# The last products of a matrix multiplication: a new order, C21's last part in two column halves, stores by halves on two queues

**The chip, the cores and the metric.** One core of one Trainium2 chip. The metric is device microseconds of one execution, as the median of several runs. The profile of one execution adds the span, from the first to the last instruction, which is about 1.8 us shorter than the time. TensorE is called PE in profile lines, VectorE DVE, ScalarE ACT, GpSimd POOL and SyncE SP; a q behind a name (SPq) is the sequencer of that engine, which waits, branches and issues DMAs.

## The reference

```python
"x": np.random.randn(8, 2048, 2048).astype(np.float32)
"w": np.random.randn(2048, 2048).astype(np.float32)

cs = np.cumsum(x, axis=1)
diff = cs - np.concatenate([zeros, cs[:, :-1, :]], axis=1)   # zeros: one row
return np.matmul(diff, w).astype(np.float32)
```

The difference of the cumulative sum is x again up to rounding, so the kernel computes x @ w.

## The kernel before

The product is done by a Strassen-like scheme with seven products in place of eight, twice nested: blocks A11 … S4 of x against B11 … T4 of w, and inside the last outer product a second level with products `a11 t11` … `s3 Q3`. A product of the inner level is four matmuls of 512 columns into one PSUM bank. ScalarE moves a first result to the output tile with a scale (`keep`), VectorE adds the further ones (`add`).

```python
    def product_in(ps, a, b, first):
        for k in range(4):
            nc.tensor.matmul(
                ps, a[k], b[k], start=(first and k == 0), stop=(k == 3), skip_group_check=True
            )
    ...
    def keep(dst, ps, scale):     # ScalarE: dst = ps * scale
    def add(dst, ps, scale):      # VectorE: dst = ps * scale + dst
    ... (bodies cut)

        def four_last():
            a11, a12, a22, s1, s2, s3, s4 = A4
            Q1, Q2, Q4, t11, Q3, t21, t22 = in4
            C21g, C21h = new_c(b), new_c(c)
            product_in(q, a11, t11, True)
            keep(C21g[:, :NB], q, vg)
            product_in(X[0], a12, t21, False)
            add(C21g[:, :NB], X[0], vg)
            product_in(X[1], s4, t22, False)
            keep(C21g[:, NB:], X[1], vg)
            product_in(e, s1, Q1, True)
            add(C21g[:, NB:], e, vg)
            keep(C21h[:, NB:], Y[1], vh)
            add(C21h[:, NB:], e, vh)
            product_in(q, s2, Q2, False)
            add(C21g[:, NB:], q, vg)
            put(C21g, g + 1, 0)
            product_in(Y[0], a22, Q4, False)
            keep(C21h[:, :NB], Y[0], vh)
            product_in(q, s3, Q3, False)
            for n in range(2):
                at = ds(n * NB, NB)
                add(C21h[:, at], q, vh)
                nc.scalar.dma_start(out2[ds((h + 1) * P, P), at], C21h[:, at])
```

`four_last` is the last function to run. q, e, X[0], X[1], Y[0] and Y[1] are PSUM banks; X and Y already hold partial sums. NB is 512, P is 128. Two early places matter later: seven output stores of 256 KB are issued on GpSimd's queue, at 59 to 64 us, and nine on SyncE's, at 74 to 80 us (the recorded expectations say "about 100 us"):

```python
        with tc.issue_after(whole_max.ins):
            for c, rows, columns in done:
                put(c, rows, columns)                                  # GpSimd's queue
        ...
        for c, rows, columns in done:
            after("sp", lambda: put(c, rows, columns, nc.sync))        # SyncE's queue
```

## Time and profile before

| | kernel before |
|---|---|
| time, median of 3 (lowest to highest) | 1509.28 us (1508.52 to 1510.85) |
| span of the profiled execution | 1507.3 us, granted clock 1.0 (the share of TensorE's full speed that it was given) |
| TensorE, VectorE, ScalarE busy | 99%, 73%, 57% |
| start of the first product of `four_last`, a11 t11 | 1495.56 us |

I measure the end of the kernel from the start of a11 t11, since everything ahead of it is the same in both kernels. This row of TensorE's timeline (start, length, operation, count) sets that zero; it holds a11 t11 and the next product:

```profile
1495.56 1.89 PE L479 MATMUL b<-W,xT 128*128 128x512 f16 x8
```

From there to the end of the span it is 11.8 us, called the *tail* below, 0.8% of the span. The part of it after the last store has landed I call the *closing*.

### The profile page before, as it was taken

The numbers are of one execution on the slowest core, as the hardware profiler recorded it, in microseconds if no ns is written. First come the engines' busy times: TensorE is split into PE (matmuls) and PEld (weight loads), VectorE is DVE, ScalarE is ACT, GpSimd is POOL, SyncE is SP. The second block draws the span as 40 slices with busy tenths as digits, with TensorE's granted clock in tenths as the row PEclk, the third lists the DMA queues.
The fourth block names the chain that finished last, engine by engine and source line by source line (L and its number), as shares of the span: only waits on it lengthen the run. The fifth ranks groups of instructions, "written<-read, shape, count | busy, mean of one in ns | idle before, by whom it ended". The sixth has DMA issues, their size and how long they took to land.

```text
span 1507.3 us, 19123 instructions
## 1 busy us (share of the span) xinstructions
PE 1490.6 (99%) x6911; PEld 673.8 (45%) x6911; DVE 1104.4 (73%) x2053; ACT 864.5 (57%) x1107; POOL 5.2 (0%) x12
## 2 busy tenths in 40 slices
PE   8999999999999999999999999999999999999998
PEld 3444444444444444444444444444444444444443
DVE  7997777776677676777676776766776767776767
ACT  5875655565655566555656555655555565556551
POOL 0100000000000000000000000000000000000000
PEclk9999999999999999999999999999999999999999
DMA  9988878878978987888789788878788888887772
GB/s 362 351 250 233 236 224 246 234 213 227 235 225 244 224 224 236 215 246 236 210 229 232 230 241 217 235 222 248 216 244 207 236 221 250 232 236 216 223 208 112
DMA packets 322479, 351.50 MB, mean 233 GB/s; under 512 B 266896, under 2 KB 266896, under 8 KB 306512
## 3 DMA queue, kind: packets, MB, share of 16 engines
q1 hardware_dynamic: 321536, 347.92, 81.1%
q0 software_dynamic: 560, 1.84, 0.3%
q8 instruction: 54, 0.88, 0.2%
q10 hardware_dynamic: 288, 0.52, 0.1%
q14 instruction: 41, 0.34, 0.1%
HBM read 150.99 MB, written 134.22 MB: 189 GB/s over the span
## 4 chain that ended last, share of the span: by engine, by line
PE 88%; DVE 1%; DMA 1%; issue 0%; ACT 0%; DVEq 0%; ACTq 0%; SPq 0%
PE b L468 52%; PE b L479 36%; DVE c L502 1%; DMA fin<-in_x_dram 0%; DMA xT<-fin 0%; DVE W L511 0%; ACT b L553 0%; DVE W L515 0%; ACT c L497 0%; DVEq L937 0%; DVE xT L511 0%; DVE s L112 0%; DVE m L111 0%; DVE u L586 0%; DVE m L561 0%
## 5 line engine op out<-in xcount | busy, mean ns | idle before, releaser
L502 DVE SCALAR_TENSOR_TENSOR c<-b,u,c 128x512 f32<-128x512 f32 (+1 forms) x883 | 675.0, 799 | 234.8 <-ACT c L497 112.8
L497 ACT ACTIVATE c<-b,u 128x512 f32<-128x512 f32 x496 | 314.5, 680 | 265.4 <-PE b L468 170.5
L468 PE MATMUL b<-W,xT 128*128 128x512 f16 x2048 | 462.1, 379 | 0.8 <-ACT c L497 0.8
L468 PE MATMUL b<-W,W 128*128 128x512 f16 x1764 | 411.7, 379 | 1.8 <-ACT c L497 1.5
L105 ACT ACTIVATE c<-fin 128x2048 f16<-128x2048 f32 x92 | 175.7, 1910 | 242.4 <-DMA out_dram<-c 220.5
L468 PEld LDWEIGHTS <-xT 128*128 128x128 f16 x2048 | 200.4, 98 | 242.6 <-issue 1.1
L468 PEld LDWEIGHTS <-W 128*128 128x128 f16 x2016 | 197.2, 98 | 240.2 <-issue 2.1
L116 ACT ACTIVATE fin<-fin,s 128x2048 f16<-128x2048 f32 x123 | 246.3, 2002 | 93.8 <-issue 50.8
L479 PEld LDWEIGHTS <-W 128*128 128x128 f16 x1560 | 152.1, 98 | 187.5 <-issue 2.5
L479 PE MATMUL b<-W,W 128*128 128x512 f16 x810 | 220.0, 379 | 1.0 <-DVE c L502 1.0
L479 PE MATMUL b<-W,xT 128*128 128x512 f16 x720 | 180.0, 379 | 0.0
L479 PE MATMUL b<-inner,W 128*128 128x512 f16 x660 | 176.2, 379 | 0.0
L479 PEld LDWEIGHTS <-xT 128*128 128x128 f16 x960 | 93.9, 98 | 113.3
L561 DVE TENSOR_REDUCE m<-m 128x1 f32<-128x4 f32 x29 | 4.6, 157 | 106.7 <-ACT b L553 106.7
L553 ACT ACTIVATE b<-fin 128x512 f32<-128x512 f32 x116 | 67.8, 585 | 14.5 <-DMA fin<-in_x_dram 14.5
L468 PE MATMUL b<-W 128*128 128x512 f16 x252 | 75.0, 379 | 0.0
L511 DVE TENSOR_TENSOR W<-W,xT 128x1024 f16<-128x1024 f16 x122 | 68.2, 559 | 3.2
L511 DVE TENSOR_TENSOR W<-xT,W 128x1024 f16<-128x1024 f16 x122 | 67.5, 553 | 0.0
L479 PE MATMUL b<-inner,xT 128*128 128x512 f16 x240 | 61.6, 379 | 0.0
L233 PE MATMUL b<-wb,xP 128*128 128x512 bf16 x240 | 55.4, 383 | 5.9 <-ACT wb L216 4.8
L511 DVE TENSOR_TENSOR W<-xT,xT 128x1024 f16<-128x1024 f16 (+1 forms) x92 | 54.8, 596 | 0.0
L111 DVE TENSOR_SCALAR m<-m 128x1 f32<-128x1 f32 x124 | 18.5, 149 | 34.6 <-ACT c L105 33.5
(54 smaller groups left out, 457.9 us busy)
## 6 DMA issues: line engine op xcount, KB each, us to landing
out_dram<-c SPq DMA_DIRECT2D x247, 512.0 KB, 3.1
fin<-in_x_dram SPq DMA_DIRECT2D x123, 1024.0 KB, 5.5
W<-in_w_dram SPq DMA_DIRECT2D x32, 512.0 KB, 9.6
W<-in_x_dram SPq DMA_DIRECT2D x16, 256.0 KB, 7.4
xT<-fin SPq DMA_TRANSPOSE x184, 5.2
out_dram<-o POOLq DMA_DIRECT2D x7, 256.0 KB, 3.9
out_dram<-o SPq DMA_DIRECT2D x7, 256.0 KB, 4.1
xP<-in_x_dram SPq DMA_DIRECT2D x1, 1024.0 KB, 5.1
```

The source lines that it names most:

```text
L105: return m, nc.scalar.activation(waste.bitcast(f16), xf, ABS, scale=1.0 / ROW, accum_out=m)
L111: nc.vector.tensor_scalar(m, m, TINY, None, MAX)
L116: return xh, nc.scalar.activation(xh, xf, COPY, scale=s)
L233: lambda: nc.tensor.matmul(ps[r][n], xP[:, r, ko, :], wb[h, ko][:, ds(n * NB, NB)], start=(ko == 0), stop=(ko == KO - 1),),
L468: nc.tensor.matmul(ps[n], a[k], b[k][:, n, :], start=(first and k == 0), stop=(k == KH - 1), skip_group_check=True,)
L479: nc.tensor.matmul(ps, a[k], b[k], start=(first and k == 0), stop=(k == 3), skip_group_check=True)
L497: after("act", lambda: nc.scalar.activation(c, p, COPY, scale=scale))
L502: "dve", lambda: nc.vector.scalar_tensor_tensor(c, p, scale, c, MUL, ADD)
L511: after("dve", lambda: nc.vector.tensor_tensor(dst.all, p.all, q.all, op))
L553: lambda: nc.scalar.activation(ps[i % 2], xf[:, at], ABS, scale=1.0 / ROW, accum_out=m4[:, i : i + 1],),
L561: after("dve", lambda: nc.vector.tensor_reduce(m, m4, AX.X, ADD))
```

## The change

Its intent: when the last product is done, little should be left to add and to store. Q4 comes last, cut into two column halves in two banks, so that the last add and store are of 256 columns. The banks are reused later than before, so TensorE need not wait for them. C21g is stored by halves, and the last stores go through two queues.

```diff
             product_in(X[0], a12, t21, False)
             add(C21g[:, :NB], X[0], vg)
-            product_in(X[1], s4, t22, False)
-            keep(C21g[:, NB:], X[1], vg)
+            out_of(C21g, g + 1, ds(0, NB), nc.sync)
+            product_in(q, s2, Q2, False)
+            keep(C21g[:, NB:], q, vg)
             product_in(e, s1, Q1, True)
+            one, two = (ds(n * NB // 2, NB // 2) for n in range(2))
+            keep(C21h[:, two], Y[0][:, two], vh)
+            keep(C21h[:, NB:], Y[1], vh)
+            product_in(X[1], s4, t22, False)
             add(C21g[:, NB:], e, vg)
-            keep(C21h[:, NB:], Y[1], vh)
             add(C21h[:, NB:], e, vh)
-            product_in(q, s2, Q2, False)
-            add(C21g[:, NB:], q, vg)
-            put(C21g, g + 1, 0)
-            product_in(Y[0], a22, Q4, False)
-            keep(C21h[:, :NB], Y[0], vh)
+            add(C21g[:, NB:], X[1], vg)
+            out_of(C21g, g + 1, ds(NB, NB), nc.sync)
             product_in(q, s3, Q3, False)
-            for n in range(2): ...           # two adds of q, two stores of 256 KB on ScalarE's queue
+            keep(C21h[:, one], q[:, one], vh)
+            add(C21h[:, NB:], q, vh)
+            add(C21h[:, two], q[:, two], vh)
+            out_of(C21h, h + 1, ds(NB, NB), nc.scalar)
+            for at, ps, queue in (one, Y[0], nc.sync), (two, X[0], nc.scalar):
+                product_in(ps[:, at], a22, [b[:, at] for b in Q4], ps is X[0])
+                add(C21h[:, at], ps[:, at], vh)
+                out_of(C21h, h + 1, at, queue)
```

(The bodies of the old loop and of `out_of`, which is one `dma_start`, are cut.)

More of the change, by code (lines that the diff above doesn't have):

```diff
@@ L875, in four_last, with out_of @@
             C21g, C21h = new_c(b), new_c(c)
+            def out_of(c, t, at, queue):
+                queue.dma_start(out2[ds(t * P, P), at], c[:, at])
             product_in(q, a11, t11, True)
@@ L879, in four_last @@
             add(C21g[:, :NB], X[0], vg)
+            out_of(C21g, g + 1, ds(0, NB), nc.sync)
+            product_in(q, s2, Q2, False)
+            keep(C21g[:, NB:], q, vg)
+            product_in(e, s1, Q1, True)
+            one, two = (ds(n * NB // 2, NB // 2) for n in range(2))
+            keep(C21h[:, two], Y[0][:, two], vh)
+            keep(C21h[:, NB:], Y[1], vh)
             product_in(X[1], s4, t22, False)
-            keep(C21g[:, NB:], X[1], vg)
-            product_in(e, s1, Q1, True)
             add(C21g[:, NB:], e, vg)
-            keep(C21h[:, NB:], Y[1], vh)
             add(C21h[:, NB:], e, vh)
-            product_in(q, s2, Q2, False)
-            add(C21g[:, NB:], q, vg)
-            put(C21g, g + 1, 0)
-            product_in(Y[0], a22, Q4, False)
-            keep(C21h[:, :NB], Y[0], vh)
-            product_in(q, s3, Q3, False)
-            for n in range(2):
-                at = ds(n * NB, NB)
-                add(C21h[:, at], q, vh)
-                nc.scalar.dma_start(out2[ds((h + 1) * P, P), at], C21h[:, at])
+            add(C21g[:, NB:], X[1], vg)
+            out_of(C21g, g + 1, ds(NB, NB), nc.sync)
+            product_in(q, s3, Q3, False)
+            keep(C21h[:, one], q[:, one], vh)
[6 more added lines that the diff above has]
+                out_of(C21h, h + 1, at, queue)
         inner_product(A3, in3, banks, C12g, C12h, *u, between_3)
```

## The prediction

> **What bounds the kernel now.** I read the page first, to see which engine sets the span, and then only the end, because the change touches nothing but the last function that runs.
>
> The page's busy shares and its chain of waits:
>
> ```profile
> PE 1490.6 (99%) x6911; PEld 673.8 (45%) x6911; DVE 1104.4 (73%) x2053; ACT 864.5 (57%) x1107; POOL 5.2 (0%) x12
> ...
> PE 88%; DVE 1%; DMA 1%; issue 0%; ACT 0%; DVEq 0%; ACTq 0%; SPq 0%
> ```
>
> TensorE (PE) is busy in 99% of 1507.3 us and carries 88% of the chain. The change neither adds nor removes matmul columns (below), so the first 1495 us stay as they are, and what can be won lies after TensorE's stream thins out. The chain from 1495 us on shows where that is (start, length, what):
>
> ```profile
> 1495.72 3.47 PE b L479 x16
> ...
> 1499.28 0.06 DVE c L502
> 1499.34 0.61 issue
> 1499.95 0.14 DVE c L502
> 1500.09 0.51 issue
> 1500.61 0.75 DVE c L502
> 1501.36 0.04 issue
> 1501.40 1.04 PE b L479 x4
> ...
> 1502.53 0.75 DVE c L502
> ```
>
> At 1499.28 the chain leaves TensorE for VectorE (DVE): three adds start 0.66 to 0.67 us apart, and the third must finish reading bank q before the last product, s3 Q3, may accumulate into the same bank. Then come four matmuls, and the final adds. The timelines of TensorE, VectorE and ScalarE (ACT) over the same stretch give starts and lengths:
>
> ```profile
> 1497.29 1.03 PE L479 MATMUL b<-W,W 128*128 128x512 f16 x4
> 1498.15 1.89 PE L479 MATMUL b<-inner,W 128*128 128x512 f16 x8
> 1499.88 1.03 PE L479 MATMUL b<-inner,xT 128*128 128x512 f16 x4
> 1501.40 0.38 PE L479 MATMUL b<-W,W 128*128 128x512 f16 x1 [0.50 <-DVE c L502]
> ...
> 1499.28 2.07 DVE L502 SCALAR_TENSOR_TENSOR c<-b,u,c 128x512 f32<-128x512 f32 x3 [0.81 <-PE b L479]
> 1502.53 1.41 DVE L502 SCALAR_TENSOR_TENSOR c<-b,u,c 128x512 f32<-128x512 f32 x2 [1.18 <-PE b L479]
> ...
> 1496.62 0.69 ACT L497 ACTIVATE c<-b,u 128x512 f32<-128x512 f32 x1 [9.33 <-PE b L479]
> 1498.35 1.26 ACT L497 ACTIVATE c<-b,u 128x512 f32<-128x512 f32 x2 [1.04 <-PE b L479]
> 1500.94 0.69 ACT L497 ACTIVATE c<-b,u 128x512 f32<-128x512 f32 x1 [1.32 <-PE b L479]
> 1503.32 1.00 ACTq L895 DMA_DIRECT2D out_dram<-c  x2
> ```
>
> The bracket of 0.50 us is TensorE waiting for bank q, 1.18 us is VectorE waiting for the last product. VectorE ends at 1502.53 + 1.41 = 1503.94; the second store of 256 KB is issued at 1504.0 (1503.98 from the row of 1.00 us less the 0.34 of one issue). The stores' own view says how long a store takes to land, and the table of stretches when bytes move:
>
> ```profile
> DMA to landing us min/median/max: 2.4/2.4/2.5
> ...
> 1504.00:1506.00 2.00, 0.00 (x0) 0.00 (x0) 0.00 (x0) 0.00 (x0) 0.00 (x0) 1.00 0.68 262
> 1506.00:1507.30 1.30, 0.00 (x0) 0.00 (x0) 0.00 (x0) 0.00 (x0) 0.00 (x0) 0.76 0.00 0
> ```
>
> From 1504.0 no engine works: 3.3 us, 0.22% of the span, is the last store's flight and the program's end. The last one lands at 1503.98 + 2.4 = 1506.4, so some 0.9 us are the closing of the program after it. A finer cut of that view shows the two last stores' bytes moving from about 1504.2 to 1505.6 at some 390 GB/s: 0.67 us for each 256 KB, one after the other.
>
> **What the Trainium skill says.** (1) "PSUM — Partial Sum Buffer", The four PSUM rules: a first matmul clears the written marks of its whole 2 KiB bank, not only of the columns it writes. So the second column half needs a bank of its own when it starts afresh; the change takes X[0], already read. Same page, PSUM bank collisions raise a hardware error: two engines must not be in one bank at once, reads against reads included. The build agrees: the add of q into C21h's right half waits for ScalarE too, though its other operand was settled an add earlier. No run yet shows what that wait costs. (2) "TensorE: Matmul & The Clock Gate", Back-to-back issue gap: N/2.4 + 2.5 ns warm, so 216 ns at 512 columns and 109 ns at 256. The trace agrees at 512: 16 matmuls in 3.62 us, less 0.38 for the last, is 216 ns each. Eight 128-column transposes, each with its own weight load, take 0.61 us, 56 ns apart, so weight loads won't hold 256-column matmuls to more than that. (3) "VectorE: DVE Perf Modes", Why PSUM operands drop a tier: fp32 from PSUM runs at one element a cycle. The trace agrees: adds of 1024 columns take 1272 ns, of 512 take 746, so 1.03 ns a column and 220 ns fixed; a 256-column add is then 0.48 us. (4) "DMA: Bandwidth & Descriptors", Anatomy of one DMA: about 2 us of a DMA are fixed, mostly the write receipt. Landing in 2.4 us with 0.67 us of bytes leaves 1.7 fixed here, for this path.
>
> **The change part by part.** Times are on the old kernel's clock. Columns of matmul: four of 512 in Q4 become eight of 256, the same sum; there are four more weight loads, overlapped. TensorE work saved: none.
>
> a) *Order.* s2 Q2 moves from fifth product to third, so it follows a keep of q by ScalarE, not an add by VectorE. That keep ends at 1496.62 + 0.69 = 1497.31; the matmuls would start at 1497.29, and the old trace shows a release 0.04 us after the reader's end (1501.36 to 1501.40). So they start at 1497.35: +0.06 us. Product e ends as fourth in both orders; its first add moves from 1499.28 to 1499.34.
>
> b) *The wait of TensorE goes.* Starts at four matmuls of 0.216 each: s2 1497.35, e 1498.21, s4 1499.08, s3 1499.94, the two halves of Q4 (four of 0.109) 1500.81 and 1501.24. Before s3, q must have been read: ScalarE keeps s2 from 1498.41 to 1499.10, so no wait. All results are there at 1501.56 + 0.27 = 1501.83 (the tail of a 256-column matmul is my estimate, 0.38 less 0.11), against 1502.05 + 0.38 = 1502.43 in the old kernel. TensorE gains 0.6 us.
>
> c) *ScalarE.* Five keeps in place of four: 512, 512, 256, 512, 256 columns. Starts 0.58 us apart for 512 (1.26 for two). A half is about 0.47 long, 0.37 apart, from 0.83 ns a column (1059 ns for 1024 columns, 1910 for 2048). They end at 1497.31, 1499.10, 1499.5 and 1500.05; the last, of q's left quarter, needs s3, whose last matmul ends at 1500.97, so 1501.02 to 1501.50.
>
> d) *VectorE.* Five last adds (e, e, q, q, q, of 512) become seven: four of 512 and three of 256. After e at 1499.34: the second e waits for the keep of Y[1] (1500.05) and starts at 1500.13; X[1] at 1500.79; q into the right half could start at 1501.46 but waits for ScalarE to leave the bank (1501.50), so 1501.56; then three halves, started 1502.22, 1502.62 and 1503.02 (0.66 after a full one, 0.40 after a half: 0.48 less the same 0.08 overlap). The last ends at 1503.50. Against 1503.94 that is −0.44 us. VectorE has taken TensorE's place: from 1500.8 it runs without a gap while the last product has been ready since 1501.83. That is why the gain is below TensorE's 0.6 plus the shorter last add.
>
> e) *Stores.* The last one has 128 KB, not 256: 0.33 us less of bytes at 390 GB/s. C21g's second half is issued at 1501.5 and C21h's right half at 1502.3, so their bytes are gone by 1503.8; the left quarters follow at 1503.1 on one queue and at 1503.54 on the other. Rows become 1 KB, for which this trace has no record; I put 0.05 us on them. Landing 2.4 − 0.33 + 0.05 = 2.1 us, so 1505.65, plus the 0.9 us of closing: span 1506.55.
>
> Sum: −0.44 (end of VectorE) − 0.28 (shorter last store) = −0.7 to −0.8 us. The predicted time is 1509.28 − 0.8 = **1508.5 us**.
>
> **Rivals.** *VectorE isn't the bound, and the end follows TensorE:* the last half would be added at 1501.93 and finished at 1502.4, a gain of 1.5 at the adds and 0.3 at the store, so 1507.5. Against it: adds of 3 × 0.66 + 3 × 0.40 must still pass after the add of X[1] and cannot start before s4 is done at 1500.1. *The store is hidden anyway:* the end may hang on the closing of the program, or the receipt may not shrink with size; then only the 0.44 remains: 1508.8. For it: 1.7 of the 2.4 us are fixed. *Two queues and small rows cost:* an extra 256-column store, interleaved with the other one in the same DMA engines, could take what it saves; with the 0.44 used up too, 1509.3. *The new waits on ScalarE are longer than worked out,* because five keeps lie on the path of two engines: a keep late by 0.3 us moves VectorE by 0.3, so 1508.8; a whole gain lost gives 1509.3. I see nothing that adds more than 1 us, since every wait of the new order is one keep or one add long.
>
> **Range and chances.** The mechanism is worth 0 to 1.8 us over the rivals, with 0.8 in the middle. The three old runs lie 2.33 us apart (1508.52 to 1510.85), more than the whole effect, and a median of few runs carries perhaps half of that. So the range is **1507.2 to 1509.7**. Two per cent is 30 us, nine times all the time between the last add and the end; no rival comes near: faster 0.005, same 0.99, slower 0.005.
>
> **What would show it.** In the new trace: TensorE's bracket of 0.50 us for VectorE gone, at most 0.1 us for ScalarE before s2; VectorE's last seven adds nearly gapless from 1500.1, the last ending at about 1503.5; 256-column adds of 0.48 us; the add of q released by ScalarE, not TensorE; the last store landing in 2.1 us; the last landing to the span's end 0.9 us. I'm wrong if VectorE has gaps behind TensorE at the end, if the small store lands no sooner than 2.4 us, or if the span falls by more than 1.8 us or not at all. A change before 1495 us would be scatter, not the change.

## The result, and the profile after

The changed kernel took 1509.33 us (median of 3, 1508.78 to 1510.5) against 1509.28. The ratio is 1.000, with a 95% interval of 0.9977 to 1.0023. By the clock on the wall nothing happened. The trace shows that something did.

The timelines of the changed kernel, first TensorE, then VectorE, then ScalarE with its stores:

```profile
1495.68 1.89 PE L479 MATMUL b<-W,xT 128*128 128x512 f16 x8
1497.49 1.89 PE L479 MATMUL b<-inner,W 128*128 128x512 f16 x8
1499.21 1.24 PE L479 MATMUL b<-W,W 128*128 128x512 f16 x5
...
1500.94 1.04 PE L479 MATMUL b<-inner,xT 128*128 128x256 f16 x8
...
1499.48 4.09 DVE L502 SCALAR_TENSOR_TENSOR c<-b,u,c 128x512 f32<-128x512 f32 x7 [0.88 <-PE b L479]
...
1498.55 1.63 ACT L497 ACTIVATE c<-b,u 128x512 f32<-128x512 f32 x3 [1.11 <-PE b L479]
1501.14 0.47 ACT L497 ACTIVATE c<-b,u 128x256 f32<-128x256 f32 x1 [0.96 <-PE b L479]
1502.43 1.51 ACTq L878 DMA_DIRECT2D out_dram<-c  x2
```

TensorE's bracket of 0.50 us is gone, and its last matmul ends 0.6 us earlier against a11 t11. The seven adds stand in one row of 4.09 us: VectorE runs to 1503.57 with hardly a pause, while the last product was ready at 1501.98. The chain of waits says the same:

```profile
1499.13 1.06 ACT c L497 x2
1500.19 0.02 issue
1500.21 0.08 DVE c L502
1500.29 0.59 issue
1500.88 0.75 DVE c L502
...
1501.64 1.20 DVE c L502 x3
```

It leaves TensorE for ScalarE's keeps, and then stays on VectorE to the end of the adds. Its starts show two waits that the merged row of adds hides. The third add starts 0.67 us after the second (1500.88 less 1500.21), which is what an add takes that waits for nothing. The second starts 0.73 after the first, and the fourth, of q, 0.76 after the third (1501.64 less 1500.88). Both start 0.03 us after the end of a keep by ScalarE; that of q ends at 1501.14 + 0.47 = 1501.61. So ScalarE holds VectorE up by 0.07 and 0.10 us.

Then the stores: the view of DMAs gives size and time to landing of the last two, and for SyncE the view of the closing line, cut to the time after the last landing, gives its instructions (the second line is the same view cut once more, at 1506.15, ahead of the final barrier):

```profile
out_dram<-c SPq DMA_DIRECT2D x1, 128.0 KB, 2.1
out_dram<-c ACTq DMA_DIRECT2D x1, 128.0 KB, 2.1
...
L947 SPq EVENT_SEMAPHORE  x9: 17/28/28, 1505.7 to 1506.9; - x9
...
L947 SPq EVENT_SEMAPHORE  x7: 27/28/28, 1505.7 to 1506.1; - x7
```

The same view of the kernel before:

```profile
L937 SPq EVENT_SEMAPHORE  x3: 17/17/28, 1506.5 to 1507.3; - x3
```

This is the line that explains where a third of a microsecond went. Of the instructions after the last landing, two belong to the barrier that ends the program in both kernels. Before, one other remains: the check of the semaphore of that last store. In the changed kernel there are seven others, from 1505.74 to 1506.11, so one every 0.06 us. The DMAs that SyncE and ScalarE issue take eight landing semaphores in rotation, and at the program's end SyncE checks these in a fixed order, one after the other. Before, the two last stores had the two that are checked last; with two stores more, they have the first and the second, and six checks of stores that landed earlier come after: 6 times 0.06 is the 0.36 us.

| from the start of a11 t11, us | before | changed | difference |
|---|---|---|---|
| last add ends | 8.39 | 7.89 | −0.50 |
| last store issued | 8.42 | 7.92 | −0.50 |
| last store landed | 10.89 | 10.04 | −0.85 |
| end of the span (tail) | 11.78 | 11.30 | −0.48 |
| closing (the last row less the one above) | 0.90 | 1.26 | +0.36 |

The change saved 0.85 us up to the last landing and lost 0.36 of it in the closing. The remaining half microsecond is 0.03% of the time. Scatter hides it: in the thirteen traces a11 t11 starts between 1494.70 and 1496.54 us.

### The profile page after: what moved, and what is told of

Its sections match the earlier page's. It is cut to its first block, busy times and chain, and to the rows that moved or that the text cites. A ratio compares the mean times of both kernels' runs of the same rounds, so it can differ in the third digit from the quotient of the medians.

```text
span 1507.0 us, 19138 instructions
## 1 busy us (share of the span) xinstructions
PE 1490.6 (99%) x6915; PEld 674.2 (45%) x6915; DVE 1105.1 (73%) x2055; ACT 865.1 (57%) x1108; POOL 5.0 (0%) x12
## 4 chain that ended last, share of the span: by engine, by line
PE 88%; DVE 1%; DMA 1%; ACT 0%; issue 0%; DVEq 0%; ACTq 0%; SPq 0%
PE b L468 52%; PE b L479 35%; DVE c L502 1%; DMA fin<-in_x_dram 0%; DMA xT<-fin 0%; DVE W L511 0%; ACT b L553 0%; DVE W L515 0%; ACT c L497 0%; DVEq L947 0%; DVE xT L511 0%; DVE s L112 0%; DVE m L111 0%; DVE u L586 0%; DVE m L561 0%
## 5 line engine op out<-in xcount | busy, mean ns | idle before, releaser
L502 DVE SCALAR_TENSOR_TENSOR c<-b,u,c 128x512 f32<-128x512 f32 (+2 forms) x885 | 675.5, 798 | 235.5 <-ACT c L497 115.1
L497 ACT ACTIVATE c<-b,u 128x512 f32<-128x512 f32 (+1 forms) x497 | 315.2, 680 | 267.0 <-PE b L468 172.5
L116 ACT ACTIVATE fin<-fin,s 128x2048 f16<-128x2048 f32 x123 | 246.3, 2002 | 94.3 <-issue 52.5
L479 PE MATMUL b<-inner,xT 128*128 128x512 f16 (+1 forms) x244 | 61.6, 376 | 0.0
```

The costliest lines, as they stand in the source:

```text
L116: return xh, nc.scalar.activation(xh, xf, COPY, scale=s)
L479: nc.tensor.matmul(ps, a[k], b[k], start=(first and k == 0), stop=(k == 3), skip_group_check=True)
L497: after("act", lambda: nc.scalar.activation(c, p, COPY, scale=scale))
L502: "dve", lambda: nc.vector.scalar_tensor_tensor(c, p, scale, c, MUL, ADD)
```

## The experiments

**Theory.** After the order is changed, VectorE's queue bounds the adds; and the end of the program also hangs on which landing semaphores the last stores have. **Rivals:** the longer closing is scatter or belongs to the two queues; the column halves are what shortens the tail; storing earlier helps by itself. All times below are in us from the start of a11 t11, in one trace each; the two repeats moved a tail by 0.02 at most. "Checks" are SyncE's semaphore instructions after the last landing.

| run | last add ends | last landing | checks | closing | tail | time, median (runs) |
|---|---|---|---|---|---|---|
| before | 8.39 | 10.89 | 3 | 0.90 | 11.78 | 1509.28 (3) |
| changed | 7.89 | 10.04 | 9 | 1.26 | 11.30 | 1509.33 (3) |
| changed, again | 7.88 | 10.03 | 9 | 1.25 | 11.28 | 1509.35 (5) |
| changed, two fewer early DMAs | 7.88 | 10.02 | 3 | 0.89 | 10.92 | 1507.44 (5) |
| the same, again | 7.89 | 10.04 | 3 | 0.90 | 10.94 | 1508.04 (5) |
| before, two more early DMAs | 8.38 | 10.90 | 9 | 1.25 | 12.15 | 1508.77 (5) |
| before, two fewer early DMAs | 8.38 | 10.90 | 5 | 1.02 | 11.91 | 1508.75 (6) |
| order alone | 7.58 | 10.28 | 3 | 0.90 | 11.18 | 1508.88 (5) |
| one queue | 7.89 | 10.03 | 9 | 1.26 | 11.30 | 1508.53 (1) |
| stores alone | 8.38 | 10.85 | 10 | 1.32 | 12.17 | 1509.84 (1) |
| no column halves | 7.58 | 10.09 | 3 | 0.90 | 10.99 | 1508.87 (1) |
| quarters in one bank | 7.71 | 10.22 | 3 | 0.88 | 11.10 | 1507.85 (4) |
| a further order | 7.58 | 10.26 | 3 | 0.90 | 11.15 | 1508.04 (5) |

The kernel before, run beside them, had medians of 1509.14 us (beside the changed kernel again, its two fewer, two more, and the order alone) and 1509.38 us (beside the others). The granted clock was 0.999 or 1.0 in all.

### Is the longer closing real?

The changed kernel a second time, without an edit.

> The changed kernel a second time, to see what repeats. Tail = from the start of product a11 t11 to the end of the span: 11.8 us in the kernel before, 11.3 us in the changed one. My theory (VectorE bounds the tail, and the end also hangs on SyncE's walk through the landing semaphores): tail 11.3 again within 0.1, last landing some 10.1 us after the start of a11 t11, then 1.25 us of closing with nine SyncE semaphore instructions after that landing. Rival (the closing of 1.25 us against 0.9 in the kernel before is scatter of one execution): closing anywhere from 0.9 to 1.3. Time: within 0.2% of before, not resolved.

Everything repeats to 0.02 us: nine checks, closing 1.25. Its time was 0.9999 of before's (0.9987 to 1.0012). The closing is not scatter.

### Two fewer and two more DMAs, far from the tail

To move the rotation of the semaphores without touching the tail, two early stores change queues. DMAs that GpSimd issues aren't part of this rotation: in the traces they have semaphores of their own. The moved stores go out at 67.2 and 68.9 us here, and at 51.2 and 52.5 us in the opposite edit.

```diff
-        for c, rows, columns in done:
-            after("sp", lambda: put(c, rows, columns, nc.sync))
+        for i, (c, rows, columns) in enumerate(done):
+            if i < 2:
+                put(c, rows, columns)                 # GpSimd's queue
+            else:
+                after("sp", lambda: put(c, rows, columns, nc.sync))
```

> The changed kernel, but two of the early output stores (at about 100 us) go through GpSimd's queue, so two fewer DMAs take part in the round-robin of eight landing semaphores and the two last stores get the two that SyncE looks at last, as in the kernel before. Theory: nothing else moves in the tail; after the last landing SyncE has three semaphore instructions left instead of nine, closing 0.9 us instead of 1.25, tail 10.9 us instead of 11.3. Rival (two queues, or small rows, make the closing longer): closing stays 1.25, tail 11.3. Second rival (scatter): closing anything. Time: within 0.2% of before.

The opposite in the kernel before:

```diff
-            for c, rows, columns in done:
-                put(c, rows, columns)
+            for i, (c, rows, columns) in enumerate(done):
+                put(c, rows, columns, nc.sync if i < 2 else nc.gpsimd)
```

> The kernel before, with two of the early stores moved from GpSimd's queue to SyncE's, so that its two last stores get the first two landing semaphores of the round-robin. Theory: last landing unmoved (10.9 us after the start of a11 t11), nine SyncE semaphore instructions after it instead of three, closing 1.25 us instead of 0.9, tail 12.15 us instead of 11.8. Rival (the closing belongs to the changed kernel's two queues): closing 0.9, tail 11.8. Time: within 0.2% of before.

The same view of the closing line after the last landing, first for the changed kernel with two fewer:

```profile
L950 SPq EVENT_SEMAPHORE  x3: 17/17/28, 1504.8 to 1505.6; - x3
```

then for the kernel before with two more:

```profile
L937 SPq EVENT_SEMAPHORE  x9: 17/28/28, 1505.9 to 1507.1; - x9
```

Both tails moved by 0.36 to 0.38, each in the expected direction, while last add and last landing stood still. The rival of the two queues falls: the kernel before has one queue at its end and gets the long closing too. This is as direct as it gets: stores issued more than 1400 us earlier decide 0.37 us at the end.

### The order of products alone

Q4 last but whole, C21g stored whole, the two last stores as before, so no DMA more:

```diff
             product_in(q, s3, Q3, False)
+            keep(C21h[:, :NB], q, vh)
+            add(C21h[:, NB:], q, vh)
+            (store of the right half, ScalarE's queue)
+            product_in(Y[0], a22, Q4, False)
+            add(C21h[:, :NB], Y[0], vh)
+            (store of the left half, ScalarE's queue)
```

(ahead of it the order of the changed kernel)

> The new order of products alone: Q4 last but in one piece of 512 columns, C21g stored whole, the two last stores of 256 KB on ScalarE's queue as before, as many DMAs as before. My theory (VectorE's queue bounds the tail, so the column halves only add fixed cost to it): five adds of 512 in place of four of 512 and three of 256; last add ends 7.6 us after the start of a11 t11 (8.4 before, 7.9 changed), last landing 2.4 us after its issue, closing 0.9 us, tail 11.0 us: better than the changed kernel's 11.3. Rival (the halves are what shortens the tail, the last product bounds it): last add no earlier than 8.2, tail 11.5 or more.

The last add ends at 7.58, 0.31 earlier than with the column halves, since five adds of 512 columns cost VectorE less than four of 512 and three of 256. The tail is 11.18, shorter than the whole change's 11.30, though not the 11.0 expected: the last store took 2.66 to land, because the 512 KB of C21g were just ahead of it. The two closings differ, though: up to the last landing the whole change is 0.24 ahead (10.04 against 10.28), and it is behind only by its closing. VectorE's timeline of this run:

```profile
1499.73 2.07 DVE L502 SCALAR_TENSOR_TENSOR c<-b,u,c 128x512 f32<-128x512 f32 x3 [0.88 <-PE b L479]
1502.11 1.41 DVE L502 SCALAR_TENSOR_TENSOR c<-b,u,c 128x512 f32<-128x512 f32 x2 [0.31 <-ACT c L497]
```

The bracket of 0.31 is new and worth a look: the add of q into the right half does not need anything that ScalarE writes at that moment. It waits for ScalarE to leave the bank, and starts 0.03 us after that keep ends. From start to start, this add is 0.39 us late. In the changed kernel the keep is shorter (0.47 in place of 0.69), and the same add is only 0.10 late. That the bank is the reason, and not the tile C21h, is inferred: the keep writes the other half of C21h, and the trace shows it waiting for TensorE's semaphore alone.

### One queue

```diff
-            for at, ps, queue in (one, Y[0], nc.sync), (two, X[0], nc.scalar):
+            for at, ps, queue in (one, Y[0], nc.scalar), (two, X[0], nc.scalar):
```

> The changed kernel, but both last quarters are stored on ScalarE's queue; the landing semaphores are those of the changed kernel. Theory (order of SyncE's walk): nothing moves, last add ends 7.9 us after the start of a11 t11, last landing 10.0, nine semaphore instructions and 1.25 us of closing, tail 11.3: the second queue is worth nothing, since the two stores are issued 0.4 us apart and an issue takes 0.34. Rival (a second queue at the end costs closing time, or saves issue time): closing back to 0.9 and tail 10.9, or the last landing 0.3 later and tail 11.6.

Not one figure of the table's tail moves by more than 0.01 (in one run of unknown state). The second queue is worth nothing here.

### The stores alone

In the old order of products, C21g by halves and the last two stores on two queues.

```diff
+            (store of C21g's left half after its last add)
-            put(C21g, g + 1, 0)
+            (store of C21g's right half)
-                nc.scalar.dma_start(out2[ds((h + 1) * P, P), at], C21h[:, at])
+                (nc.sync, nc.scalar)[n].dma_start(out2[ds((h + 1) * P, P), at], C21h[:, at])
```

> The stores' part of the change alone, in the old order of products: C21g by halves, the two last stores on two queues, both still 256 KB. Theory: the last add stays at 8.4 us after the start of a11 t11, the last landing at 10.9, and because there is one DMA more, the last store gets the semaphore that SyncE looks at first: ten of its semaphore instructions follow, closing 1.3, tail 12.2, so 0.4 us longer than before. Rival (storing earlier and on two queues shortens the end by itself): landing 10.6 or earlier, tail 11.5 or less.

As expected, the tail gets longer, 12.17 against 11.78: the last landing gains 0.04, and one DMA more turns three checks into ten.

### Without column halves

The order alone, with C21g by halves and one early DMA fewer, so that the semaphores of the last stores are those looked at last.

```diff
-            put(C21g, g + 1, 0)
+            (store of C21g's left half after its last add, of its right half here)
-            if i < 2:                                # in the early edit above
+            if i < 1:
```

> The new order with Q4 undivided, C21g stored by halves, and one fewer early DMA so that the last two stores have the semaphores looked at last. It differs from the run with two fewer DMAs by the column halves (and their quarter stores) alone. The run of the order alone had its last landing 2.66 us after its issue, since 512 KB of C21g went out just ahead; with halves I expect 2.4. Theory (halves lengthen VectorE's queue by about as much as the smaller store saves): last add ends 7.6 us after the start of a11 t11 against 7.9, last landing 10.0 in both, closing 0.9, tail 10.9, as with halves. Rival (halves do pay): tail 11.1 or more.

The tail is 10.99, against 10.92 and 10.94 with the halves and the same closing. So the halves are worth 0.06 or so, by two effects that nearly cancel: the last add ends 0.30 later, and the last store lands 2.10 after its issue in place of 2.48. My "worth nothing" is close, and the rival's 0.2 or more is not there. Against the order alone, C21g by halves brings 0.19.

### Two attempts at a better tail

The first: product e second (the expectation says third; the edit has it second), s3 ahead of s4, so that VectorE has work where it idled; the last add and store cut into quarters; two early DMAs fewer.

```diff
+            product_in(q, a11, t11, True)     # then e: s1 Q1; q: s2 Q2; X[0]: a12 t21;
+            ...                               # q: s3 Q3; X[1]: s4 t22; Y[0]: a22 Q4
+            for n, queue in enumerate((nc.sync, nc.scalar)):
+                at = ds(n * NB // 2, NB // 2)
+                add(C21h[:, at], Y[0][:, at], vh)
+                out_of(C21h, h + 1, at, queue)
```

> A version meant to beat both: e third and s3 before s4, so that VectorE has work in its idle stretch, Q4 undivided, its add and store in two column quarters, ScalarE keeping the whole left half of s3, and two fewer early DMAs for the semaphores. Theory (VectorE's queue bounds the tail): last add ends 7.6 us after the start of a11 t11 (7.9 changed, 8.4 before), its store has 128 KB, last landing 9.8, closing 0.9, tail 10.7, 1.1 us below before's 11.8. Rival (TensorE's last product bounds): the product ends at 6.4 and the last add no earlier than 7.4 anyway, so a tail of 10.5. Time: scatter between executions ahead of the tail is 1.8 us in the four traces so far, so I expect 1507 to 1509 us and no verdict beyond same.

The last add ended at 7.58 as expected, and the tail is 11.15, not 10.7. The view of DMAs shows why; the last three stores by size and time to landing:

```profile
out_dram<-c SPq DMA_DIRECT2D x1, 256.0 KB, 2.7
out_dram<-c SPq DMA_DIRECT2D x1, 128.0 KB, 2.8
out_dram<-c ACTq DMA_DIRECT2D x1, 128.0 KB, 2.6
```

The small stores take longer than in the changed kernel (2.1), since C21g's right half now goes out late and its bytes stand ahead of theirs. A VectorE that finishes earlier doesn't help when the bytes queue.

The second keeps the run without column halves and cuts only the last add and store:

```diff
-            add(C21h[:, :NB], Y[0], vh)
-            nc.scalar.dma_start(out2[ds((h + 1) * P, P), ds(0, NB)], C21h[:, :NB])
+            for n, queue in enumerate((nc.sync, nc.scalar)):
+                at = ds(n * NB // 2, NB // 2)
+                add(C21h[:, at], Y[0][:, at], vh)
+                queue.dma_start(out2[ds((h + 1) * P, P), at], C21h[:, at])
```

> The run without column halves, but with its last add and store cut into two quarters of 256 columns; the product stays one of 512 columns in one bank, and two fewer early DMAs set the semaphores. Theory: last add ends 7.7 us after a11 t11 (0.14 later than uncut, 0.16 earlier than with the product cut), the last store lands 2.15 us after its issue, at 9.9, closing 0.9, tail 10.8: cutting the add and the store pays a little, cutting the product does not. Rival (bytes queue behind the earlier stores, as in the new order that failed): landing 10.1, tail 11.0.

It missed in the same way. Its stores:

```profile
out_dram<-c ACTq DMA_DIRECT2D x1, 256.0 KB, 2.4
out_dram<-c SPq DMA_DIRECT2D x1, 128.0 KB, 2.6
out_dram<-c ACTq DMA_DIRECT2D x1, 128.0 KB, 2.4
```

The rival held: landing 10.22. ScalarE's keep of 512 columns holds the bank longer, the right half's store is issued at 6.96 in place of 6.75, and the two quarters queue behind it. Here the column halves of the change do help, by making that keep short.

The traces hold a simpler reading, which no run tests by itself. Look at the store with which the last 512 KB of output begin, and at the last landing: 7.76 and 10.89 before, 6.75 and 10.04 changed, 6.96 and 10.28 in the order alone, 6.96 and 10.22 here. In twelve of the thirteen traces these are 3.10 to 3.32 us apart, whatever was done to the last add; the new order has 3.44. An estimate from the figures of the old trace: 512 KB at 390 GB/s take 1.34 us, and with 1.7 us fixed that is 3.04. So the bytes bound the last landing almost as closely as the last add does, and what moved it by 0.85 us goes with the earlier issue of that store, by 1.01.

### Is a faster time real?

The kernel before with the early edit of two fewer, and the best version repeated.

> The kernel before with the early edit alone (two of the stores at about 100 us through GpSimd's queue), since the changed kernel with that edit came out 1.7 us faster than before in the medians and its tail accounts for 0.9 of that. Theory (the rest is scatter): the stretch up to a11 t11 within the range of the other traces, 1494.7 to 1496.5 us; last landing 10.9 us after a11 t11, five semaphore instructions after it, closing 1.0, tail 11.9; time as before within 0.1%. Rival (the edit itself shortens the first 1495 us): a11 t11 at 1494.8 or earlier and a median of 1508.4 or less, 0.06% below before.

> The changed kernel with two fewer early DMAs, repeated: is its 0.13% real? Theory (tail of 10.9 against 11.8 us, and the rest scatter): tail 10.9 again, closing 0.9, median 0.9 us below before's, 0.05 to 0.07%. Rival (the first median was luck): median within 0.5 us of before's. Second rival (the early edit shortens the front): 1.7 us below again, and the run of before with that edit alone is faster too.

The tails are as expected in both: 11.91 with five checks, and 10.94. The times don't settle. The changed kernel with two fewer had ratios of 0.9987 (0.9975 to 1.0000) and 0.9989 (0.9976 to 1.0003), medians 1.7 and 1.3 us below before's; the tail accounts for 0.9. The kernel before with the same edit had 0.9993 (0.9980 to 1.0005), 0.6 below with a tail 0.1 longer. That hints at some half microsecond gained ahead of the tail by the early edit, but the opposite edit came out 0.4 below before too, with a tail 0.4 longer. It stays open whether the early edit does anything to the first 1495 us. By the tail alone, the changed kernel with two fewer early DMAs is the best version of all: 10.9 against 11.8 before and 11.3 as changed.

## Why the prediction was right or wrong

It gave 1508.5 us in a range of 1507.2 to 1509.7, and "the same" with 0.99; the measured 1509.33 lies inside. The range also holds "no change at all" (1509.28), so lying inside it confirms little; the trace has to. The verdict rests on the right ground, that a tail of 12 us cannot move 1509 by 2%. Point by point:

- *(a) The order costs 0.06 at s2.* Measured 0.08: the third product starts 1.804 after a11 t11, where the old order had 1.727.
- *(b) TensorE's wait goes.* The last matmul ends at 6.29, expected 6.27 (1501.83 less 1495.56); before 6.87.
- *(c) ScalarE's keeps.* The half keeps took 0.47, as worked out, and the last ended at 5.93, expected 5.94.
- *(d) VectorE bounds the tail.* The last add ended at 7.89, expected 7.94. The chain of waits confirms the ground, and the run of the order alone too: fewer adds, an earlier end. That ScalarE and not TensorE releases the add of q came true: it starts 0.03 us after ScalarE's keep and 0.10 us late, as worked out (1501.46 put off to 1501.56); the order alone shows it with 0.31 us of idle time. The Trainium skill's remark in "PSUM — Partial Sum Buffer", PSUM bank collisions raise a hardware error, that reads against reads count, thus has a price in this case. VectorE bounds the last add, but not the landing alone: the order alone ended its adds 0.31 earlier and landed 0.24 later.
- *(e) The store.* 2.1 us to landing, as worked out. The last landing came 0.85 earlier, expected 0.75. (The old kernel's last store took 2.47 by itself; the prediction used the median of two, 2.4.)
- *The step that failed* is the last term of (e), "plus the 0.9 us of closing". I took the closing as a constant of the program. It measured 1.26, since the change adds two DMAs and so moves its last stores to semaphores that SyncE looks at first. The two runs that moved nothing but the rotation show it in both directions. So of the 0.7 to 0.8 expected the tail got 0.48.
- *The rivals.* "The store is hidden anyway" came out nearest by its number: a gain of 0.44 against 0.48 of tail. That is luck: the small store did land sooner (2.1 us against 2.47), and the closing took the difference. "Two queues cost" fell: one queue is the same to 0.01. Against the first rival the prediction counts 3 × 0.66 + 3 × 0.40 us of adds "after the add of X[1]"; that count runs from the second add of e. From the start of X[1]'s add it is 2 × 0.66 + 3 × 0.40. The rival fails either way: the last add ended 1.6 us after the last product.
- *What the prediction did not ask:* which part of the change pays. The order alone, with less code, gives 0.60 of tail against 0.48 for the whole; the whole change's added stores take back 0.36 in the closing.

The median 0.8 us above the predicted one is not explained by the closing alone (0.36). The rest is within the scatter between executions, and no run here separates it; nor does any show the 0.48 in the time.

## What to carry to other kernels

Behind a last product, count what the adding engine still has in its queue: cutting a product into halves shortens the last add but lengthens the queue by a fixed cost each (here seven adds ended 0.31 us after five). Treat the end of the program as part of the tail: look at how many semaphore checks stand after the last landing, since in this program the number of DMAs in the rotation, wherever they are issued, decides it. And compare traces from a common point near the change, because a half microsecond doesn't show in medians that scatter by two.

## What the Trainium skill lacked or had wrong

- No page that I looked up has it (nearest: "DMA: Bandwidth & Descriptors", Queues, rings and completion order): the order of the waits at a program's end. Here the landing semaphores are checked one after the other at 0.06 us each, in a fixed order, so the closing after the last landing was 0.9 to 1.3 us by the number of checks left (3, 5, 9 and 10 gave 0.90, 1.02, 1.26 and 1.32).
- "PSUM — Partial Sum Buffer", PSUM bank collisions raise a hardware error: it names the hazard of two readers, not the cost of the wait that keeps them apart. An add started 0.39 us late (0.31 of it idle) behind a keep of 512 columns, and 0.10 late behind one of 256.
- "DMA: Bandwidth & Descriptors", Anatomy of one DMA: its fixed 2.0 us plus bytes is given for the path through GpSimd. Stores from SyncE and ScalarE landed in 2.1 us (128 KB) and 2.3 to 2.4 us (256 KB) with little ahead of them, and in up to 2.8 us (128 KB) behind others.
- "TensorE: Matmul & The Clock Gate", Back-to-back issue gap: it says that in a real stream of weight loads and matmuls of 512 columns the spacing is about 131 ns, and that N/2.4 + 2.5 over-counts. This kernel is such a stream and measured 216 ns, the formula's value (the prediction quoted the formula without this remark); with 256 columns, eight matmuls in 1.04 us are 110 ns apart (1.04 less 0.27 for the last), the formula's 109.
